# Feed-forward steps in another order, and three weight units cast by one operation

## The chip, the cores and the metric

The kernel runs on one core of one Trainium2 chip. The time is that of one execution on the device, in microseconds; the median of three executions is given, and beside it one execution was recorded by the profiler.

## The reference

One encoder block for 256 tokens of 2048 channels, all in float32. Two branches (gated linear attention and a Hyena convolution) are computed from one input projection, gated, merged, projected and normalised. Then comes the part that matters here, a squared-ReLU MLP of width 8192 and a second normalisation:

```
h = _layernorm(DEEPNORM_ALPHA * h + mix, ln1_g[l], ln1_b[l])
ff = jnp.square(jax.nn.relu(h @ w_ff1[l])) @ w_ff2[l]
h = _layernorm(DEEPNORM_ALPHA * h + ff, ln2_g[l], ln2_b[l])
```

## The kernel before

All weights stream from HBM in blocks of 128 x 2048 float32 (1 MB). TensorE works in a reduced float32 format, so each operand is taken as a high part (a cast on ScalarE, `cast`, L1103) and a low part (raw minus high, on VectorE, `rest`, L1106), and a product is three matmuls: high by high, high by low, low by high. In the table of the profile these casts stand under L1104 and all VectorE operations of the stage under L1101, the lines of the two helpers.

The MLP's hidden width is taken in four quarters of 2048. `ff1_first` computes the first quarter of h @ w_ff1. `ff_pairs` (L1278) then runs 48 steps; step s does one block of w_ff1 for a later quarter (16 blocks of 128 hidden channels make one quarter) and one block of w_ff2 for the quarter before it. Product with w_ff2 goes by a Strassen-Winograd scheme on 2 x 2 blocks: seven products in place of eight. The seven accumulators `w` lie in seven of the eight PSUM banks for 8 steps each; then their sums are added to the result in SBUF (`take_sum`, L1251, on ScalarE for the first quarter's, else on VectorE), and when the quarters for one half of the columns are done, eight additions join them (`join_sums`, L1262). The eighth bank holds the ff1 result `f` of the step.

What a step works on:

- A block of w_ff2, in one of three tiles of a ring, is four units u0 to u3 of 512 columns. `plain_split` (L1156) takes the high and low part of u0 to u2 as they are (the names b_h, b_l). Then VectorE adds u0 += u3 and u3 = u0 + u1, and GpSimd issues two DMAs that accumulate into the tile: u1 += (u3's columns once more from HBM, L1169) and u2 += u3 (L1170). `pair_split` (L1183) splits units 0 and 3, `last_split` (L1187) units 1 and 2, which the DMAs have changed (into the spare columns of the two fa tiles). So each block gives seven weight pieces: three plain, two of the pair, two of the last.
- `form_products` (L1238) does the three matmuls per piece, against the seven forms of the hidden activations in the fa tiles.
- A block of w_ff1, in one of two `fraw` tiles, is split in two halves (`half_split`, L1201), whose 2 x 12 weight loads and matmuls, of 512 and 256 columns, go into `f` (L147, L151). `quad_sum` (L1109) adds the two parts of `f` into a tile of hidden activations, one such tile for two steps: ScalarE copies one part (f_l), VectorE adds. After the second step `squares` (L1117) applies ReLU and square on ScalarE.
- `forms` (L1123) makes the seven forms of one activation tile with their high and low parts: on VectorE a chain of small differences and low parts, on ScalarE three casts that wait for them. They overwrite the fa slots when the quarter that used them is done with that slot.

High and low tiles of weights rotate over three buffers, which pair, half 0 and half 1 take in turn; the tiles of the plain units, of the last units and the `f` bank exist once.

The order within a step is written out by hand: `pin` keeps the instructions of an engine in the order of the program text. What is not pinned (the loads, the joins, the rest) a scheduler places; on SP's queue stand by turns the ring load of block p, which waits for the low part of `last_split(p - 3)`, and the fraw load of block p, which waits for half 1 of block p - 2. `quad_sum` and `take_sum` have high priority. In step s the text goes: products of the three plain pieces; `plain_split(s + 1)`; products of the pair; f half 0; `half_split(s + 1, 0)`; `pair_split(s + 1)`; products of the last pieces of step s - 1; `last_split(s)`; the load of a ring tile; f half 1; `quad_sum`; `half_split(s + 1, 1)`, which also issues the load of the next fraw block; `forms` in steps 9 to 16 of each 16; `squares` in odd steps. Ring and fraw loads are issued on SP's queue, the accumulating DMAs on GpSimd's. A sum is taken directly behind the last matmuls of its accumulator, in `form_products`.

Of the kernel before, what the change touches and what calls it, by code (L numbers as in the profile page):

```python
# [9 lines left out]
F32 = mybir.dt.float32  # L10
# [6 lines left out]
P = 128  # L17
# [26 lines left out]
def block_kernel(  # L44
# [93 lines left out]
    def channel_psum(name):  # L138
        return psum_main(name).rearrange("p (a b) -> p a b", a=2)
# [109 lines left out]
    with tc.tile_pool(name="xp", bufs=1) as xp, tc.tile_pool(name="xq", bufs=1) as xq:  # L249
        def units(pool, tag, n, **kw):  # L250
            t = pool.tile([P, n, OPENING * P], F32R, tag=tag, name=f"open_{tag}", **kw)
            return lambda a, b: t[:, a:b].rearrange("p k (b j) -> p k b j", b=OPENING)
# [713 lines left out]
    rows1 = load_rows(0)  # L966
    turn_b, turn_i = dfth, dftl
    for i, t in ((0, turn_b), (1, turn_i)):
        raw = ep.tile([P, 1024], F32, tag="wx", name=f"turn{i}")[:, 0:512].rearrange("p (a b) -> p a b", b=P)
        nc.scalar.dma_start(raw, ln_turn[i])  # L970
        nc.scalar.copy(t, raw)
        if i == 0:
            nc.vector.tensor_tensor(t[32:64], raw[32:64], t[32:64].bitcast(F32), op=ALU.subtract)
# [7 lines left out]
    for g in range(3):  # L981
        pss = token_group(mT, f"wo{g}")
        for tb in range(NT):
            add_mix(pss[tb], tb, g * 512, 512)
    x0 = tuple(ep.tile([P, D], F32R, tag=t, name=t) for t in ("xh", "xl"))
    parts = resident([x0] + halves(ep, "f", "wr1"))
    pss = [[psum_main(f"wo3_{tb}{ch}") for ch in range(2)] for tb in range(NT)]
    column_products(pss, mT, [queue.popleft()], range(NT), 0)
# [40 lines left out]

    def begin_three():  # L1030
        blocks = [queue.popleft(), [], []]
        hx, lx = (ep.tile([P, D], F32R, tag=t, name=f"{t}_f") for t in ("xh", "xl"))
        at = 0
        for b in (1, 2):
            n = fetched[0]
            fetched[0] = n + 1
            raw = wp.tile([P, D], F32, tag="raw", bufs=3, name=f"raw{n}")
            nc.sync.dma_start(raw, wblk[n])
            for h in range(2):
                src = raw[:, h * 1024:(h + 1) * 1024]  # L1040
                if b + h == 2:
                    hi, lo = hx[:, at:at + 1024], lx[:, at:at + 1024]
                    at += 1024
                    with tc.issue_after(scaled[0].ins):
                        nc.scalar.copy(hi, src)
                    with tc.issue_after(turned[1][1].ins):
                        nc.vector.tensor_tensor(lo, src, hi.bitcast(F32), op=ALU.subtract)
                elif b == 1:
                    hi, lo = weight_half(n, h)
                    split_hi_lo(hi, lo, src)  # L1050
                else:
                    hi, lo = n, src
                blocks[b].append((hi, lo))
        begun = [(channel_psum(f"f0_{b // 2}_{b % 2}"), parts, 1 if b == 2 else 2) for b, parts in enumerate(blocks)]
        for at, size in CHUNKS:
            for ps, parts, n in begun:
                if at // P < 8 * n:
                    high_by_tokens(ps, hT, parts[at // 1024], range(at // P, (at + size) // P), slice(0, P))
        n, src = blocks[2][1]
        blocks[2][1] = weight_half(n, 1)  # L1060
        split_hi_lo(*blocks[2][1], src)
        fetch()
        return begun
# [11 lines left out]
    def fa_slot(i):  # L1075
        if fa[1] is None:
            fa[1] = ep.tile([P, 8192], F32R, tag="f", name="fa1")
        t = fa[i // 4][:, i % 4 * 1792:(i % 4 + 1) * 1792]
        return t.rearrange("p (h k j) -> p h k j", h=2, j=P)
# [9 lines left out]
    quad_tiles = [base.tile([P, 4, P], F32, tag=t, name=f"fr{i}") for i, t in enumerate(("dfth", "dftl", "sum"))]  # L1089
    quad_tiles += [ep.tile([P, 4, P], F32, tag=f"fr{i}", name=f"fr{i}") for i in (3, 4)]  # L1090

    def quads(i):
        return quad_tiles[i % 5]

    pinned = [False]

# [6 lines left out]
    def cast(hi, src):  # L1103
        return pin(nc.scalar.copy(hi, src))  # L1104

    def rest(lo, src, hi):  # L1106
        return VT(lo, src, hi.bitcast(F32), ALU.subtract)
# [6 lines left out]
            cast(low, ps[:, 1])  # L1114
            VT(dst, halves[0], halves[1], ALU.add)

    def squares(i):  # L1117
        q = quads(i)
        pin(nc.scalar.activation(q, q, AF.Relu))
        return pin(nc.scalar.activation(q, q, AF.Square))  # L1120


    def forms(i, plain=False):  # L1123
        q, slot = quads(i), fa_slot(i)
        hi, lo = slot[:, 0], slot[:, 1]
        if plain:
            cast(hi[:, 0:4], q)
            rest(lo[:, 0:4], q, hi[:, 0:4])
            return
        t = base.tile([P, 2, P], F32, tag="as", name=f"fw{i}")  # L1130
        cast(hi[:, 0:3], q[:, 1:4])
        VT(t, q[:, 0:1].broadcast_to([P, 2, P]), q[:, 1:3][:, ::-1], ALU.subtract)
        cast(hi[:, 3:5], t)
        VT(q[:, 0], q[:, 1], t[:, 0], ALU.subtract)
        rest(lo[:, 0:3], q[:, 1:4], hi[:, 0:3])
        VT(q[:, 2], q[:, 3], q[:, 0], ALU.subtract)
        cast(hi[:, 5:7], q[:, 0:3:2])
        rest(lo[:, 3:5], t, hi[:, 3:5])
        rest(lo[:, 5:7], q[:, 0:3:2], hi[:, 5:7])
# [4 lines left out]
            return fa_slot(kt // 2)[:, part, ((1, 0), (3, 2))[kt % 2][ts.start // P]]  # L1144

    SLOTS = 48

    def ring_load(p):
        nc.sync.dma_start(ring_tile(p), wblk[FF_PAIRS + 2 * p])
# [5 lines left out]

    def plain_split(p):  # L1156
        raw, n = ring_tile(p), FF_PAIRS + 2 * p
        hi = ep.tile([P, D], F32R, tag="xh", name=f"b_h{p}")
        lo = ep.tile([P, 1024], F32R, tag="wx", name=f"b_l{p}")
        u = units(raw)  # L1160
        at = slice(0, 1024), slice(1024, 1536)
        low = lo, hi[:, 1536:2048]
        for c in at:
            cast(hi[:, c], raw[:, c])
        for c, dst in zip(at, low):
            rest(dst, raw[:, c], hi[:, c])
        VT(u[0], u[0], u[3], ALU.add)
        VT(u[3], u[0], u[1], ALU.add)
        nc.gpsimd.dma_start(u[1], wblk[n, :, 1536:2048], accum_op=ALU.add)  # L1169
        nc.gpsimd.dma_start(u[2], u[3], accum_op=ALU.add)  # L1170
        h = units(hi)
        pieces_of[p, 0] = list(zip(h[:3], units(lo) + h[3:]))

    def split_units(p, kind, hi, lo, raw):
        by_unit = [t.rearrange("p (u c) -> p u c", c=512) for t in (hi, lo)]
# [7 lines left out]
    def pair_split(p):  # L1183
        hi, lo = weight_half(FF_PAIRS + 2 * p, 0)
        split_units(p, 1, hi, lo, raw_units(p)[:, 0:4:3])
# [52 lines left out]
    def form_products(pss, p, which, ks):  # L1238
        i = p % 8
        slot = fa_slot(i)  # L1240
        for k, (wh, wl) in zip(ks, pieces_of.pop((p, which))):
            ps, f = pss[k], FORM[k]
            sh, sl = slot[:, 0, f], slot[:, 1, f]
            pin(MM(ps, sh, wh, start=(i == 0), stop=False))  # L1244
            MM(ps, sh, wl, start=False, stop=False)  # L1245
            pin(MM(ps, sl, wh, start=False, stop=(i == 7)))  # L1246
        if i == 7:
            for k in ks:
                take_sum(p // 16, p // 8 % 2, k, pss[k])

# [27 lines left out]
    def ff_pairs():  # L1278
        pss = [psum_side(f"w{j}") if j not in (2, 3, 4) else psum_main(f"w{j}") for j in range(7)]
        joins = []  # L1280
        for s in range(SLOTS):
            more = s + 1 < SLOTS
            pinned[0] = True
            form_products(pss, s, 0, (0, 1, 2))
            if more:
                plain_split(s + 1)
            form_products(pss, s, 1, (3, 4))
            ps = channel_psum(f"f{s // 16 + 1}_{s % 16}")
            channel_products(ps, hT, half_parts.pop((s, 0)), range(8))
            if more:  # L1290
                half_split(s + 1, 0)
                pair_split(s + 1)
            if s:
                form_products(pss, s - 1, 2, (5, 6))
                if s == SLOTS - 8:
                    joins = join_sums(0)
            last_split(s)
            if s + 2 < SLOTS:
                ring_load(s + 2)
            channel_products(ps, hT, half_parts.pop((s, 1)), range(8, 16))  # L1300
            i, c = divmod(s % 16, 2)
            quad_sum(i, c, ps, f"f{s // 16 + 1}_l{s % 16}")
            if more:
                half_split(s + 1, 1)
            if s >= 9 and (s - 9) % 16 < 8:
                forms((s - 9) % 16, s >= 2 * 16 + 9)
            if c:
                squares(i)
            if joins:
                joins.pop(0)()  # L1310
            pinned[0] = False
            if s == SLOTS - 2:
                stop_at[0] = nblk - 4
                fetched[0] = FF_PAIRS + 2 * SLOTS
            for _ in range(max(0, s - SLOTS + 3)):
                fetch()
        return pss, joins

    def ff_close(pss, joins):
        form_products(pss, SLOTS - 1, 2, (5, 6))  # L1320
        forms(7, True)
        for j in joins + join_sums(1):
            j()

# [25 lines left out]
    def quarters(*tiles):  # L1350
# [1 line left out]
        return [[(at[0], at[1]), (at[2], at[3])], [(at[4], at[5]), (at[6], at[7])]]  # L1352

    spare = [t[:, 7168:8192] for t in fa]
    own = [ep.tile([P, n], F32R, tag=t, name=f"{t}_r")
           for t, n in (("xh", D), ("xl", D), ("fraw", D))]
    parts = resident_pieces(quarters(*own, *spare)
                            + [[(a[:, c:c + 1024], b[:, c:c + 1024]) for c in (0, 1024)] for a, b in halves(ep, "hT", "wr3")])
    minus = ep.tile([P, P], F32, tag="minus", name="minus")
# [198 lines left out]
```

## Time and profile before

| | |
|---|---|
| median of 3 executions | 1818.28 us (1817.59 to 1818.85) |
| profiled execution | 1818.21 us |
| its span, first to last instruction | 1816.4 us |
| mean granted TensorE clock | 0.999 |
| ScalarE busy | 1042.5 us (57%) |
| GpSimd busy | 164.8 us (9%) |
| the 48 steps | from 1199.3 to 1717.4 us of the span |
| bytes moved | 424.77 MB, mean 234 GB/s |

A row of a timeline or of the chain gives a start and a duration in us, the engine, the line, the operation with its output and inputs, and in brackets the idle time before it with what ended it. PE is TensorE's matmuls, PEld its weight loads, DVE VectorE, ACT ScalarE, POOL GpSimd, SPq the queue that issues loads. A group row gives the count, busy us and mean ns of one, and behind the second bar the idle us before with what ended most of it. The matmuls of a step stand as w (L1244 to L1246) and f.

### The profile page before, as it was taken

What the parts mean: (1) busy time and instruction counts of PE and PEld (TensorE: products, weight loads), DVE (VectorE), ACT (ScalarE), POOL (GpSimd) and SP (SyncE); (2) the same over time, 40 slices, a digit from 0 to 9 for tenths busy, and PEclk for the clock granted to TensorE, in tenths of its full rate; (3) what the DMA queues carried; (4) which work ended last, traced back from release to release, by engine and by line L of the source; (5) the groups of instructions that cost most, each with busy time, mean ns of one, the idle gap of its engine ahead of it and who ended that gap; (6) DMA issues with size and microseconds to landing.
All of it is one profiled execution on the core that took longest, in us unless ns stands there. A gap on an engine that the chain in (4) does not pass through costs nothing.

```text
span 1816.4 us, 23481 instructions
## 1 busy us (share of the span) xinstructions
PE 1797.7 (99%) x8787; PEld 1505.1 (83%) x8787; DVE 1454.9 (80%) x1893; ACT 1042.5 (57%) x1423; POOL 164.8 (9%) x217
## 2 busy tenths in 40 slices
PE   9999999999999999999999999999999999999998
PEld 7888888888888888888888889888877887788887
DVE  6789887875689899988755667688889888989867
ACT  6678668865344444444544445666666566666632
POOL 1011110000111101010000000011111111111100
PEclk9999999999999999999999999999999999999999
DMA  8678876445798979797555764578777977789663
GB/s 324 227 256 292 249 230 200 149 163 204 229 297 250 308 248 283 251 278 258 197 187 186 310 235 159 187 213 248 236 227 235 275 235 221 221 255 273 214 219 127
DMA packets 79283, 424.77 MB, mean 234 GB/s; under 512 B 9817, under 2 KB 12393, under 8 KB 38465
## 3 DMA queue, kind: packets, MB, share of 16 engines
q1 hardware_dynamic: 47808, 336.61, 50.5%
q0 software_dynamic: 24304, 66.99, 18.2%
q10 hardware_dynamic: 7056, 19.67, 3.1%
q8 instruction: 69, 1.13, 0.3%
q14 instruction: 46, 0.37, 0.1%
HBM read 381.86 MB, written 16.25 MB: 219 GB/s over the span
## 4 chain that ended last, share of the span: by engine, by line
PE 87%; DVE 7%; ACT 3%; issue 3%; DMA 1%; ACTq 0%; DVEq 0%; POOL 0%
PE f L147 9%; PE f L151 5%; PE g L200 3%; PE g L199 3%; PE g L201 3%; PE ux L199 3%; PE ux L200 3%; PE ux L201 3%; PE w L1245 3%; PE w L1244 3%; PE w L1246 3%; PE k L147 2%; PE v L201 2%; PE v L200 2%; PE v L199 2%
## 5 line engine op out<-in xcount | busy, mean ns | idle before, releaser
L86 ACT CAST whi<-raw 128x1024 fp32r<-128x1024 f32 x392 | 412.7, 1055 | 408.6 <-PE ux L201 84.4
L87 DVE TENSOR_TENSOR wlo<-raw,whi 128x1024 fp32r<-128x1024 f32 x392 | 477.1, 1221 | 206.8 <-ACT whi L86 205.5
L147 PE MATMUL f<-hT,whi 128*128 128x512 f32 x984 | 246.4, 395 | 2.4 <-DVE fr L1101 1.9
L147 PEld LDWEIGHTS f<-hT,whi 128*128 128x128 f32 x984 | 180.4, 189 | 44.4 <-DVE fr L1101 10.1
L151 PEld LDWEIGHTS f<-hT,wlo 128*128 128x128 f32 x984 | 132.3, 190 | 8.7
L151 PE MATMUL f<-hT,wlo 128*128 128x256 f32 x984 | 135.0, 282 | 0.0
L1101 DVE TENSOR_TENSOR wlo<-fraw,whi 128x1024 fp32r<-128x1024 f32 x96 | 117.0, 1219 | 11.8 <-ACT whi L1104 11.8
L1169 POOL DMA_DIRECT2D ring<-wblk x48 | 41.7, 869 | 723.0 <-DVE ring L1101 723.0
L1104 ACT CAST whi<-ring 128x1024 fp32r<-128x1024 f32 x48 | 50.6, 1054 | 90.6 <-DVE ring L1101 83.8
L1104 ACT CAST whi<-fraw 128x1024 fp32r<-128x1024 f32 x96 | 100.7, 1049 | 0.2 <-PE f L147 0.2
L200 PE MATMUL g<-wlo,xT 128*128 128x512 f32 x256 | 100.1, 391 | 0.0
L201 PE MATMUL ux<-whi,xT 128*128 128x512 f32 x256 | 99.9, 390 | 0.0
L201 PE MATMUL g<-whi,xT 128*128 128x512 f32 x256 | 99.8, 390 | 0.0
L200 PE MATMUL ux<-wlo,xT 128*128 128x512 f32 x256 | 99.6, 389 | 0.0
L199 PE MATMUL g<-whi,xT 128*128 128x512 f32 x256 | 93.8, 392 | 0.0
L199 PE MATMUL ux<-whi,xT 128*128 128x512 f32 x256 | 89.7, 389 | 0.0
L1101 DVE TENSOR_TENSOR b_l<-ring,b_h 128x1024 fp32r<-128x1024 f32 x48 | 58.7, 1224 | 33.1 <-ACT b_h L1104 33.0
L1104 ACT CAST b_h<-ring 128x1024 fp32r<-128x1024 f32 x96 | 74.9, 829 | 8.8 <-ACT whi L1104 8.2
L1101 DVE TENSOR_TENSOR ring<-ring 128x512 f32<-128x512 f32 x96 | 66.0, 688 | 1.6
L1101 DVE TENSOR_TENSOR wlo<-ring,whi 128x1024 fp32r<-128x1024 f32 x48 | 58.8, 1225 | 2.7 <-ACT whi L1104 1.2
L1101 DVE TENSOR_TENSOR fa<-ring,fa 128x1024 fp32r<-128x1024 f32 x48 | 58.5, 1219 | 0.8 <-ACT fa L1104 0.8
L1104 ACT COPY f_l<-f 128x256 f32<-128x256 f32 x64 | 23.7, 370 | 61.1 <-PE f L147 58.2
(538 smaller groups left out, 4345.4 us busy)
## 6 DMA issues: line engine op xcount, KB each, us to landing
raw<-wblk SPq DMA_DIRECT2D x204, 1024.0 KB, 5.1
fraw<-wblk SPq DMA_DIRECT2D x48, 1024.0 KB, 7.1
ring<-wblk SPq DMA_DIRECT2D x48, 1024.0 KB, 6.2
Td<-T POOLq DMA_DIRECT2D x32, 384.0 KB, 5.4
conv_sb<-conv_rows SPq DMA_DIRECT2D x12, 1024.0 KB, 11.5
Tl<-Td POOLq DMA_DIRECT2D x16, 768.0 KB, 9.4
ring<-wblk POOLq DMA_DIRECT2D x48, 256.0 KB, 4.3
ring<-ring POOLq DMA_DIRECT2D x48, 256.0 KB, 5.0
```

The costliest lines, as they stand in the source:

```text
L86: return (nc.scalar.copy(hi, src), nc.vector.tensor_tensor(lo, src, hi.bitcast(F32), op=ALU.subtract))
L87: nc.vector.tensor_tensor(lo, src, hi.bitcast(F32), op=ALU.subtract))
L147: MM(ps[:, :, ts], hi[:, js], act[:, kt, :, ts], start=(kt == 0 and opens), stop=(kt == KT - 1))
L151: MM(ps[:, 0, ts], lo[:, js], act[:, kt, 0, ts], start=False, stop=False)
L199: MM(pss[tb], sh, wh, start=(kt == 0), stop=False)
L200: MM(pss[tb], sh, wl, start=False, stop=False)
L201: MM(pss[tb], sl, wh, start=False, stop=(kt == KT - 1))
L1101: return pin(nc.vector.tensor_tensor(dst, a, b, op=op))
L1104: return pin(nc.scalar.copy(hi, src))
L1244: pin(MM(ps, sh, wh, start=(i == 0), stop=False))
L1245: MM(ps, sh, wl, start=False, stop=False)
L1246: pin(MM(ps, sl, wh, start=False, stop=(i == 7)))
```

## The change

In a step the last pieces of step s - 1 are now multiplied directly behind the pair's, and both halves of f follow. Splitting goes in the order of use: plain units of step s + 1, last units of step s, pair of s + 1, half 0, half 1. The text of the ring load stands ahead of `plain_split`; the scheduler puts it on SP's queue as in the kernel before, for ring tile s + 3 as soon as VectorE has done the low part of `last_split(s)`, which was the tile's last reader, and the fraw load of block s + 3 next, behind half 1 of block s + 1. `squares` stand in even steps ahead of `forms`; `forms` of a quarter's eight tiles go, by the table FORMED, in the steps 9, 10, 12, 14, 15, 17, 18 and 20 counted from the start of a quarter, in place of 9 to 16, and those that fall behind the last step run in `ff_close`. Both stand ahead of `quad_sum` and half 1. Sums are no longer taken in `form_products` but by `take_sums`, behind the splits. The plain units' high and low part lie in one tile of 3072 columns (12 KB per partition), each made by one operation of 1536 columns where there were two, of 1024 and 512. The tile tags at other places follow: the first normalisation's two turn loads use the tag fraw, and tiles with the tag xh are made 3072 wide and cut to 2048.

```diff
@@ -1089,8 +1089,9 @@
     quad_tiles = [base.tile([P, 4, P], F32, tag=t, name=f"fr{i}") for i, t in enumerate(("dfth", "dftl", "sum"))]
     quad_tiles += [ep.tile([P, 4, P], F32, tag=f"fr{i}", name=f"fr{i}") for i in (3, 4)]
 
-    def quads(i):
-        return quad_tiles[i % 5]
+
+    def quads(n):
+        return quad_tiles[n % 5]
 
     pinned = [False]
 
@@ -1114,20 +1115,20 @@
             cast(low, ps[:, 1])
             VT(dst, halves[0], halves[1], ALU.add)
 
-    def squares(i):
-        q = quads(i)
+    def squares(n):
+        q = quads(n)
         pin(nc.scalar.activation(q, q, AF.Relu))
         return pin(nc.scalar.activation(q, q, AF.Square))
 
 
-    def forms(i, plain=False):
-        q, slot = quads(i), fa_slot(i)
+    def forms(n):
+        q, slot, plain = quads(n), fa_slot(n % 8), n >= 24
         hi, lo = slot[:, 0], slot[:, 1]
         if plain:
             cast(hi[:, 0:4], q)
             rest(lo[:, 0:4], q, hi[:, 0:4])
             return
-        t = base.tile([P, 2, P], F32, tag="as", name=f"fw{i}")
+        t = base.tile([P, 2, P], F32, tag="as", name=f"fw{n}")
         cast(hi[:, 0:3], q[:, 1:4])
         VT(t, q[:, 0:1].broadcast_to([P, 2, P]), q[:, 1:3][:, ::-1], ALU.subtract)
         cast(hi[:, 3:5], t)
@@ -1144,6 +1145,7 @@
             return fa_slot(kt // 2)[:, part, ((1, 0), (3, 2))[kt % 2][ts.start // P]]
 
     SLOTS = 48
+    FORMED = {16 * (q - 1) + s: 8 * q + i for q in range(1, 4) for i, s in enumerate((9, 10, 12, 14, 15, 17, 18, 20))}
 
     def ring_load(p):
         nc.sync.dma_start(ring_tile(p), wblk[FF_PAIRS + 2 * p])
@@ -1155,21 +1157,16 @@
 
     def plain_split(p):
         raw, n = ring_tile(p), FF_PAIRS + 2 * p
-        hi = ep.tile([P, D], F32R, tag="xh", name=f"b_h{p}")
-        lo = ep.tile([P, 1024], F32R, tag="wx", name=f"b_l{p}")
+        t = ep.tile([P, 3072], F32R, tag="xh", name=f"b{p}")
+        hi, lo = t[:, 0:1536], t[:, 1536:3072]
         u = units(raw)
-        at = slice(0, 1024), slice(1024, 1536)
-        low = lo, hi[:, 1536:2048]
-        for c in at:
-            cast(hi[:, c], raw[:, c])
-        for c, dst in zip(at, low):
-            rest(dst, raw[:, c], hi[:, c])
+        cast(hi, raw[:, 0:1536])
+        rest(lo, raw[:, 0:1536], hi)
         VT(u[0], u[0], u[3], ALU.add)
         VT(u[3], u[0], u[1], ALU.add)
         nc.gpsimd.dma_start(u[1], wblk[n, :, 1536:2048], accum_op=ALU.add)
         nc.gpsimd.dma_start(u[2], u[3], accum_op=ALU.add)
-        h = units(hi)
-        pieces_of[p, 0] = list(zip(h[:3], units(lo) + h[3:]))
+        pieces_of[p, 0] = list(zip(units(hi), units(lo)))
 
     def split_units(p, kind, hi, lo, raw):
         by_unit = [t.rearrange("p (u c) -> p u c", c=512) for t in (hi, lo)]
@@ -1244,7 +1241,9 @@
             pin(MM(ps, sh, wh, start=(i == 0), stop=False))
             MM(ps, sh, wl, start=False, stop=False)
             pin(MM(ps, sl, wh, start=False, stop=(i == 7)))
-        if i == 7:
+
+    def take_sums(pss, p, ks):
+        if 0 <= p < SLOTS and p % 8 == 7:
             for k in ks:
                 take_sum(p // 16, p // 8 % 2, k, pss[k])
 
@@ -1280,32 +1279,36 @@
         joins = []
         for s in range(SLOTS):
             more = s + 1 < SLOTS
+            n, c = divmod(s + 16, 2)
             pinned[0] = True
             form_products(pss, s, 0, (0, 1, 2))
+            form_products(pss, s, 1, (3, 4))
+            if s:
+                form_products(pss, s - 1, 2, (5, 6))
+            ps = channel_psum(f"f{s // 16 + 1}_{s % 16}")
+            for h in range(2):
+                channel_products(ps, hT, half_parts.pop((s, h)), range(8 * h, 8 * h + 8))
+            if s + 2 < SLOTS:
+                ring_load(s + 2)
             if more:
                 plain_split(s + 1)
-            form_products(pss, s, 1, (3, 4))
-            ps = channel_psum(f"f{s // 16 + 1}_{s % 16}")
-            channel_products(ps, hT, half_parts.pop((s, 0)), range(8))
+            take_sums(pss, s, (0, 1, 2))
+            last_split(s)
+            if more:
+                pair_split(s + 1)
+            take_sums(pss, s, (3, 4))
             if more:
                 half_split(s + 1, 0)
-                pair_split(s + 1)
-            if s:
-                form_products(pss, s - 1, 2, (5, 6))
-                if s == SLOTS - 8:
-                    joins = join_sums(0)
-            last_split(s)
-            if s + 2 < SLOTS:
-                ring_load(s + 2)
-            channel_products(ps, hT, half_parts.pop((s, 1)), range(8, 16))
-            i, c = divmod(s % 16, 2)
-            quad_sum(i, c, ps, f"f{s // 16 + 1}_l{s % 16}")
+            if c == 0 and s:
+                squares(n - 1)
+            if FORMED.get(s, 0) >= 8:
+                forms(FORMED[s])
+            take_sums(pss, s - 1, (5, 6))
+            quad_sum(n, c, ps, f"f{s // 16 + 1}_l{s % 16}")
             if more:
                 half_split(s + 1, 1)
-            if s >= 9 and (s - 9) % 16 < 8:
-                forms((s - 9) % 16, s >= 2 * 16 + 9)
-            if c:
-                squares(i)
+            if s == SLOTS - 7:
+                joins = join_sums(0)
             if joins:
                 joins.pop(0)()
             pinned[0] = False
@@ -1314,11 +1317,15 @@
                 fetched[0] = FF_PAIRS + 2 * SLOTS
             for _ in range(max(0, s - SLOTS + 3)):
                 fetch()
+        squares(31)
         return pss, joins
 
     def ff_close(pss, joins):
         form_products(pss, SLOTS - 1, 2, (5, 6))
-        forms(7, True)
+        take_sums(pss, SLOTS - 1, (5, 6))
+        for s in range(SLOTS, SLOTS + 8):
+            if s in FORMED:
+                forms(FORMED[s])
         for j in joins + join_sums(1):
             j()
```

More of the change, by code (lines that the diff above doesn't have):

```diff
@@ L968, in block_kernel @@
     for i, t in ((0, turn_b), (1, turn_i)):
-        raw = ep.tile([P, 1024], F32, tag="wx", name=f"turn{i}")[:, 0:512].rearrange("p (a b) -> p a b", b=P)
+        raw = ep.tile([P, D], F32, tag="fraw", name=f"turn{i}")[:, 0:512].rearrange("p (a b) -> p a b", b=P)
         nc.scalar.dma_start(raw, ln_turn[i])
@@ L984, in block_kernel @@
             add_mix(pss[tb], tb, g * 512, 512)
-    x0 = tuple(ep.tile([P, D], F32R, tag=t, name=t) for t in ("xh", "xl"))
+    x0 = tuple(ep.tile([P, n], F32R, tag=t, name=t)[:, 0:D] for t, n in (("xh", 3072), ("xl", D)))
     parts = resident([x0] + halves(ep, "f", "wr1"))
@@ L1031, in begin_three @@
         blocks = [queue.popleft(), [], []]
-        hx, lx = (ep.tile([P, D], F32R, tag=t, name=f"{t}_f") for t in ("xh", "xl"))
+        hx, lx = (ep.tile([P, n], F32R, tag=t, name=f"{t}_f") for t, n in (("xh", 3072), ("xl", D)))
         at = 0
@@ L1354, in block_kernel @@
     spare = [t[:, 7168:8192] for t in fa]
-    own = [ep.tile([P, n], F32R, tag=t, name=f"{t}_r")
-           for t, n in (("xh", D), ("xl", D), ("fraw", D))]
+    own = [ep.tile([P, n], F32R, tag=t, name=f"{t}_r")[:, 0:D] for t, n in (("xh", 3072), ("xl", D), ("fraw", D))]
     parts = resident_pieces(quarters(*own, *spare)
```

## The prediction

> Times in one step are given as t, in us after its first matmul (w<-b_h, L1244).
>
> **What bounds the kernel now.** First the page: TensorE.
>
> ```profile
> span 1816.4 us, 23481 instructions
> PE 1797.7 (99%) x8787; PEld 1505.1 (83%) x8787; DVE 1454.9 (80%) x1893; ACT 1042.5 (57%) x1423; POOL 164.8 (9%) x217
> ```
>
> The profiled run took 1818.21 us, 1.8 outside this span; the median is 1818.28, so the sum can be made on the profiled run as it stands. PE's 99% hides waits, because a matmul that waits for its weight load counts as busy. So I go next to the chain that ended last, which in the MLP's 48 steps shows either PE or VectorE.
>
> ```profile
> 1216.97 1.84 PE f L147 x8
> ...
> 1299.75 1.85 PE f L147 x8
> ...
> 1313.80 1.22 DVE fa L1101
> ...
> 1324.84 1.22 DVE fa L1101
> ...
> 1337.06 1.22 DVE fa L1101
> ...
> 1402.78 1.84 PE f L147 x8
> ...
> 1475.21 1.85 PE f L147 x8
> ...
> 1591.11 1.84 PE f L147 x8
> ...
> 1632.50 1.84 PE f L147 x8
> ...
> 1653.65 1.84 PE f L147 x8
> ```
>
> The rows on f are the second ff1 half of steps 1, 9, 18, 25, 35, 39 and 41; those on fa are the `last` low part of steps 11 to 13. The first 8 steps, dense, take 82.78: one every 10.345 us. From 1299.75 to 1402.78 lie 9 steps: 103.03 − 93.10 = 9.93 us too many. From 1475.21 to 1591.11 lie 10 (step 25 to 35): 115.90 − 103.45 = 12.45. From 1632.50 to 1653.65 lie 2: 0.46. **All that this change can win is therefore 22.8 us**: a ceiling at 1795.4. The excess stands where `forms` run (steps 9 to 16 and 25 to 32) and the quarter's sums are taken; there the period is 11.04 or 12.22, VectorE is on the chain, and every second step is longer. The table by stage gives its busy time:
>
> ```profile
> 1249.69:1260.04 10.35, 10.35 (x55) 8.86 (x53) 8.39 (x10) 5.95 (x7) 1.75 (x2) 1.00 0.88 256
> 1322.48:1333.52 11.04, 10.94 (x54) 8.69 (x53) 9.08 (x15) 8.01 (x12) 1.78 (x2) 1.00 0.78 240
> 1333.52:1345.72 12.20, 11.21 (x54) 8.70 (x53) 11.36 (x18) 6.86 (x10) 1.76 (x2) 1.00 0.72 218
> ```
>
> The columns are span, PE, PEld, DVE, ACT, POOL, clock, DMA share, GB/s. VectorE is busy 8.4 us of a plain step and (9.08 + 11.36) / 2 = 10.2 of one with `forms`, less than 10.345. So the loss is not work but VectorE standing idle in its turn; the waits of stage 1197 to 1720 say for what:
>
> ```profile
> L1101 DVE TENSOR_TENSOR b_l<-ring,b_h 128x1024 fp32r<-128x1024 f32 x47 | 57.5, 1224 | 33.1 <-ACT b_h L1104 33.0
> L1101 DVE TENSOR_TENSOR wlo<-fraw,whi 128x1024 fp32r<-128x1024 f32 x96 | 117.0, 1219 | 11.8 <-ACT whi L1104 11.8
> L147 PEld LDWEIGHTS f<-hT,whi 128*128 128x128 f32 x776 | 142.2, 190 | 37.0 <-DVE fr L1101 10.1
> L1245 PEld LDWEIGHTS w<-wlo,fa 128*128 128x128 f32 x96 | 18.0, 187 | 15.6 <-DVE wlo L1101 12.2
> ```
>
> **The change part by part.** *One operation for three units.* Two casts and two low parts of 1024 and 512 columns become one each.
>
> ```profile
> L1101 DVE TENSOR_TENSOR b_h<-ring,b_h 128x512 fp32r<-128x512 f32 x47 | 32.2, 684 | 0.0
> L1104 ACT CAST b_h<-ring 128x1024 fp32r<-128x1024 f32 x47 | 49.0, 1042 | 8.8 <-ACT whi L1104 8.2 <-ACT zr L1104 0.3 <-ACT fa L1104 0.2
> L1104 ACT CAST b_h<-ring 128x512 fp32r<-128x512 f32 x47 | 28.9, 615 | 0.0
> ```
>
> No row has 1536 columns. On VectorE 512 more columns cost 1224 − 684 = 540 ns, so 1536 take an estimated 1.76; two operations overlap their ends and took from 1253.06 to 1254.80 (timeline, below), 1.74. On ScalarE 1042 + 427 = 1.47, against at most 1.66 for the pair. Busy time is level within 0.1 a step. What moves is the start of the low part: it now waits for the whole cast, 1.47 after the cast's start instead of 1.04, 0.43 later. Bounds: −0.1 to +0.43 in each of the 24 or so steps where VectorE is behind, −2 to +10 us over the kernel. I take it in as the b wait of 0.4 in each of the 16 `forms` steps (below), 6.4, and none in the others, where the cover hides it.
>
> *The order.* A plain step of before:
>
> ```profile
> 1249.69 0.39 PE L1244 MATMUL w<-b_h,fa 128*128 128x512 f32 x1
> ...
> 1252.50 0.33 SPq L1197 DMA_DIRECT2D fraw<-wblk  x1
> ...
> 1252.86 0.39 PE L1246 MATMUL w<-whi,fa 128*128 128x512 f32 x1
> ...
> 1253.06 1.23 DVE L1101 TENSOR_TENSOR b_l<-ring,b_h 128x1024 fp32r<-128x1024 f32 x1 [0.59 <-ACT b_h L1104]
> ...
> 1254.80 1.42 DVE L1101 TENSOR_TENSOR ring<-ring 128x512 f32<-128x512 f32 x2
> ...
> 1256.92 0.87 POOL L1169 DMA_DIRECT2D ring<-wblk  x1 [8.37 <-DVE ring L1101]
> ...
> 1257.46 1.22 POOL L1170 DMA_DIRECT2D ring<-ring  x1
> 1257.49 1.05 ACT L1104 CAST fa<-ring 128x1024 fp32r<-128x1024 f32 x1
> ...
> 1258.57 1.23 DVE L1101 TENSOR_TENSOR fa<-ring,fa 128x1024 fp32r<-128x1024 f32 x1
> ...
> 1259.82 0.33 SPq L1149 DMA_DIRECT2D ring<-wblk  x1
> ```
>
> From 1249.69 to 1252.86 are 14 matmuls, 0.226 each, so 21 take 4.75 and the two ff1 halves the other 5.6, in either order: TensorE's own work costs nothing either way. In after TensorE has w0–2 until t = 2.03, w3–4 until 3.4, w5–6 until 4.75, f until 10.3. ScalarE then does the b cast from 2.25 (its tile is read until 2.03) to 3.7, `last` from 5.0 (its tile is read by w5–6) to 6.0, pair, half 0, squares; VectorE the b low part to 5.45, the two adds to 6.85, `last` to 8.0, pair to 9.2, half 0 to 10.4, then `forms`, the f sum, half 1. Due times: pair at 2.05 of the next step (3.2 us of cover), `last` at 3.4, half 0 at 4.75, and the f sum at 4.75, where it was 3.4 before. `Forms` and squares stand behind everything that the next matmuls need, and every second or third step has none to make up in. A `forms` step costs VectorE its 10.2 and two waits (half 1 some 0.5 behind its cast, b some 0.4): 11.0, 0.7 over. Eight of them in steps 9 to 20, and seven sums at about 0.68, are 5.6 + 4.8 = 10.4; less 3.2 of cover leaves 7.2 a quarter. The four plain steps between can give back 1.0 each (8.4 + 0.9 = 9.3 of 10.345): 3.2 left. So with transfers as fast as now the excess would be about 2 × 3.2, and following the queues instruction by instruction I get 4 to 5.
>
> SP's loads move. `fraw` goes with half 1, t = 2.8 to 3.5. The ring load goes behind `last`, which is now ahead of pair and half 0: from t = 10.13 (1259.82) to 8.05. The two accumulates are issued behind the adds: acc2 (L1170) was at 7.77, now 8.1. So **the ring load leaves together with the accumulates instead of 2.4 us behind them**. And what waits for them moves the other way: the `last` cast of the next step goes from 7.80 to 5.0. From issue to need there were 10.345 + 0.03 = 10.4 us, now 10.345 + 5.0 − 8.1 = 7.2. Behind that cast stand ScalarE's pair, half 0, the form casts and f_l, and so VectorE. How long are they under way? The page's median, and two single cases, each by the issues and the landings that the trace gives for its stretch:
>
> ```profile
> ring<-ring POOLq DMA_DIRECT2D x48, 256.0 KB, 5.0
> ```
>
> ```profile
> 1470.09 0.33 SPq L1197 DMA_DIRECT2D fraw<-wblk  x1
> ...
> 1474.34 1.22 POOL L1170 DMA_DIRECT2D ring<-ring  x1
> ```
>
> ```profile
> fraw<-wblk SPq DMA_DIRECT2D x1, 1024.0 KB, 7.1
> ```
>
> ```profile
> ring<-ring POOLq DMA_DIRECT2D x1, 256.0 KB, 7.4
> ```
>
> ```profile
> ring<-wblk SPq DMA_DIRECT2D x1, 1024.0 KB, 7.9
> fraw<-wblk SPq DMA_DIRECT2D x1, 1024.0 KB, 9.4
> ```
>
> ```profile
> ring<-ring POOLq DMA_DIRECT2D x1, 256.0 KB, 9.2
> ```
>
> The median is 5.0, with the next load 2.4 us behind. The acc2 issued at 1474.34 had a `fraw` load that left 4.25 before it and landed 1470.09 + 7.1 = 2.85 after: 7.4, 2.4 longer. The one of the last two fences left at 1412.32, with a ring load (1406.33) landing 1.9 and a `fraw` (1407.80) landing 4.9 after it: 9.2, 4.2 longer. In after every acc2 has a ring load beside it for its whole flight and a `fraw` issued 4.6 before: between 7.4 and 9.2, nearer the first, since the two loads are further apart (4.55 us instead of 2.7). I take 7.8. Then VectorE cannot catch up: from the adds of one step to the `last` low part of the next it waits for 1.24 (add's end 1256.22 to issue 1257.46) + 7.8 + 1.05 (cast) = 10.1, and a plain step takes that, giving back 0.2, not 1.0. **The excess is 2 × 7.2 = 14.4; the gain 22.8 − 14.4 = 8.4; 1818.2 − 8.4 = 1810.**
>
> The Trainium skill speaks against the change here: DMA: Bandwidth & Descriptors, Queues, rings and completion order, says that each DMA engine takes turns between its queues packet by packet, so that a load from SP holds up an accumulate from POOL as long as both have packets. The rows of 7.4 and 9.2 agree. By that rule alone acc2 would be later by the load's whole time on the engines, an estimate near 8 us, the same side of 7.2.
>
> The tiles' renaming I cost at nothing: the turn's two loads are issued before the MLP begins, the b tile was single before too, and TensorE has read it by t = 2.03, ahead of the next cast. The joins' 0.46, now behind the f sum, I count as gone.
>
> **The rivals.** *A: the accumulates stay at 5 to 6.5*, because loads that are further apart don't pile up. For it: most acc2 of before had a load in flight at one end and still took 5.0. Then the plain steps give back, the excess is 4 to 5, and the time 1818.2 − 22.8 + 4.5 = 1800. *B, slower: the accumulate's landing becomes the bound.* From 8.05 on (10.345 − 2.3) a plain step too is longer than TensorE's and loses instead of giving back; each 0.25 more costs between 2 (8 plain steps among the 24) and 6 us (all 24), I take 3. With 14.4 at 8.05 the excess passes 22.8 at 8.05 + 0.25 × 8.4 / 3 = 8.75: above that landing the change is slower. At the 9.2 of the last row the excess is 14.4 + 13.8 = 28, the time 1823.5. For it: that row, and `last` and the accumulates then run in lockstep. Against: where `last` waits, the ring load behind it waits too and moves away from the accumulates. *C: the single cast of 1536.* At its upper end, 10 instead of 6.4, it adds 4 us: 1814 with slow accumulates, at the edge of 0.2%; below nothing, 8 us less, between the forecast and A. That the order isn't as written, I give nothing: squares and `forms` stand in the queues as named.
>
> **How the numbers follow.** Forecast (acc2 7.2 to 8.2; 1805 to 1814): 0.40. A: 0.15. C, or acc2 8.2 to 8.75 (1814 to 1819): 0.22. B: 0.23. A difference under 0.2%, 3.6 us, is about what a measurement of this kernel can't tell from none: faster is below 1814.6. Faster 0.40 + 0.15 = 0.55 less a little for slow ends, 0.53; same 0.24 (C and the near end of B); slower 0.23. The range goes from A to B's price: 1799 to 1823.
>
> **What would show it.** Right: the 11.04 and 12.2 periods gone or near 10.7; the acc2 landing 7 to 8 us; a wait of the `last` cast for DMA ring<-ring, now nearly none; PEld's wait for wlo from 12.2 to under 6. A would show acc2 at 5 and the `last` cast waiting for PE w. B would show `last` waiting over 1 us for the DMA in most steps, also in plain ones, and periods over 10.345 there. Wrong altogether would be a stall at f for the f sum (L147 <- fr), now 10 us of waiting, grown; or the b low part's wait for its cast, now 33.0, on the chain.

## The result and the profile after

The changed kernel takes 1840.62 us (1839.36 to 1841.35, four runs) against 1817.99 beside it: a ratio of 1.0123, 95% interval 1.0106 to 1.0141, 22.6 us slower. The forecast was 1810.

The page of the changed kernel, span and busy time, with PE's two lines of the costliest groups:

```profile
span 1839.2 us, 23248 instructions
PE 1798.7 (98%) x8787; PEld 1506.2 (82%) x8787; DVE 1453.8 (79%) x1845; ACT 1036.1 (56%) x1375; POOL 164.9 (9%) x217
...
L147 PE MATMUL f<-hT,whi 128*128 128x512 f32 x984 | 244.9, 393 | 12.8 <-DVE fr L1102 12.8
L147 PEld LDWEIGHTS f<-hT,whi 128*128 128x128 f32 x984 | 180.0, 189 | 53.4 <-DVE fr L1102 18.8
```

No engine has more work to speak of: VectorE and ScalarE are busy 1 and 6 us less, TensorE 1 more, and the span has grown by 22.8. TensorE waits more for the f sum (12.8 us where it was 1.9), which alone would point at `forms`. The summary of waits between 1197 and 1745 us (engine, line, releaser: total, times, longest) names something that the kernel before hardly had:

```profile
ACT fa L1105 <- DMA ring<-ring: 100.1, 23, 7.8
DVE fa L1102 <- ACT fa L1105: 63.0, 22, 5.3
```

In before the first of these was 1.0 us, once. The cast of the last units waits 23 times, 4.4 us in the mean, for the second accumulate (acc2), and VectorE stands 63 us behind it. The page's table of DMA issues says why, in its last column, the median us to landing:

```profile
fraw<-wblk SPq DMA_DIRECT2D x48, 1024.0 KB, 5.6
ring<-wblk SPq DMA_DIRECT2D x48, 1024.0 KB, 7.2
...
ring<-wblk POOLq DMA_DIRECT2D x48, 256.0 KB, 5.5
ring<-ring POOLq DMA_DIRECT2D x48, 256.0 KB, 8.4
```

acc2 went from 5.0 to 8.4, the first accumulate (acc1) from 4.3 to 5.5, the ring load from 6.2 to 7.2; only `fraw` came down, 7.1 to 5.6. But a median hides the shape. Of 47 landings 12 took 6 us or less and 14 took 9.5 or more. The timeline around steps 14 and 15 (start, length, engine; the bracket is idle time and its releaser) shows one of each kind:

```profile
1347.76 0.87 POOL L1167 DMA_DIRECT2D ring<-wblk  x1 [13.49 <-issue]
...
1348.24 0.33 SPq L1151 DMA_DIRECT2D ring<-wblk  x1
1348.30 1.22 POOL L1168 DMA_DIRECT2D ring<-ring  x1
...
1352.06 0.33 SPq L1194 DMA_DIRECT2D fraw<-wblk  x1
...
1352.32 0.39 PE L1243 MATMUL w<-fa,fa 128*128 128x512 f32 x1
...
1355.68 0.87 POOL L1167 DMA_DIRECT2D ring<-wblk  x1 [6.16 <-issue]
1356.22 1.22 POOL L1168 DMA_DIRECT2D ring<-ring  x1
1359.10 1.05 ACT L1105 CAST fa<-ring 128x1024 fp32r<-128x1024 f32 x1 [7.38 <-DMA ring<-ring]
...
1360.18 1.22 DVE L1102 TENSOR_TENSOR fa<-ring,fa 128x1024 fp32r<-128x1024 f32 x1 [5.04 <-ACT fa L1105]
```

The landings of that stretch, acc1, ring load and acc2, as the trace gives them:

```profile
ring<-wblk POOLq DMA_DIRECT2D x1, 256.0 KB, 7.6
ring<-wblk SPq DMA_DIRECT2D x1, 1024.0 KB, 6.6
ring<-ring POOLq DMA_DIRECT2D x1, 256.0 KB, 10.7
```

The three leave within 0.54 us. acc1 lands at 1347.76 + 7.6 = 1355.4, half a microsecond behind the ring load (1348.24 + 6.6 = 1354.8); acc2 is caught by the `fraw` load of 1352.06 as well and lands at 1359.0. ScalarE has stood for it 7.38 us, with the pair's cast and all else behind it.

The trace of before held this case once, just ahead of the steps. The accumulates of block 0 had a ring load right behind them, and landed as late:

```profile
1188.02 0.90 POOL L1169 DMA_DIRECT2D ring<-wblk  x1 [289.12 <-DVE ring L1101]
1188.58 1.24 POOL L1170 DMA_DIRECT2D ring<-ring  x1
1188.64 0.33 SPq L1149 DMA_DIRECT2D ring<-wblk  x1
```

```profile
ring<-wblk POOLq DMA_DIRECT2D x1, 256.0 KB, 7.6
ring<-ring POOLq DMA_DIRECT2D x1, 256.0 KB, 9.2
```

Since in the changed kernel the ring load waits for the low part of `last`, the stall holds it back too: in its timeline above the accumulates of 1355.68 have no ring load beside them and landed 5.9 and 6.5 us later. So steps come in turns, one dense and one long, by the table by stage (span, PE, PEld, DVE, ACT, POOL, clock, DMA share, GB/s):

```profile
1347.79:1358.12 10.33, 10.33 (x55) 8.86 (x54) 7.29 (x8) 3.93 (x5) 3.48 (x4) 1.00 0.88 246
1358.12:1372.40 14.28, 12.50 (x55) 9.92 (x54) 11.33 (x16) 10.30 (x14) 0.45 (x1) 0.88 0.65 191
```

Added up over steps 1 to 46, the excess over 10.345 us is 22.9 in before and 45.1 in after: the 22 us that were lost. The granted clock of 0.88 in the second row stands in two steps of after (this one and step 39) and in one of before (step 32). It is worth an estimated (1 − 0.88) × 14.28 = 1.7 us in such a step, so about that much of the 22. The chain that ended last reaches back only to 1635 us in after (11% of the span), and goes through the transfer itself:

```profile
1674.09 11.59 DMA ring<-ring
1685.78 1.05 ACT fa L1105
1686.85 1.01 DVE fa L1102
...
1697.34 9.58 DMA ring<-ring
```

### The profile page after: what moved, and what is told of

It reads as the page before. It is cut to its first block, busy times and chain, and to the rows that moved or that the text cites. A ratio compares the mean times of both kernels' runs of the same rounds, so it can differ in the third digit from the quotient of the medians.

```text
span 1839.2 us, 23248 instructions
## 1 busy us (share of the span) xinstructions
PE 1798.7 (98%) x8787; PEld 1506.2 (82%) x8787; DVE 1453.8 (79%) x1845; ACT 1036.1 (56%) x1375; POOL 164.9 (9%) x217
## 5 line engine op out<-in xcount | busy, mean ns | idle before, releaser
L87 DVE TENSOR_TENSOR wlo<-raw,whi 128x1024 fp32r<-128x1024 f32 x392 | 477.4, 1221 | 206.0 <-ACT whi L86 204.4
L147 PE MATMUL f<-hT,whi 128*128 128x512 f32 x984 | 244.9, 393 | 12.8 <-DVE fr L1102 12.8
L147 PEld LDWEIGHTS f<-hT,whi 128*128 128x128 f32 x984 | 180.0, 189 | 53.4 <-DVE fr L1102 18.8
L151 PEld LDWEIGHTS f<-hT,wlo 128*128 128x128 f32 x984 | 126.1, 191 | 4.8
L151 PE MATMUL f<-hT,wlo 128*128 128x256 f32 x984 | 127.7, 283 | 0.0
L1102 DVE TENSOR_TENSOR wlo<-fraw,whi 128x1024 fp32r<-128x1024 f32 x96 | 117.1, 1219 | 12.2 <-ACT whi L1105 12.2
L1105 ACT CAST fa<-ring 128x1024 fp32r<-128x1024 f32 x48 | 50.4, 1050 | 128.4 <-DMA ring<-ring 100.1
L1102 DVE TENSOR_TENSOR fa<-ring,fa 128x1024 fp32r<-128x1024 f32 x48 | 58.6, 1221 | 63.0 <-ACT fa L1105 63.0
L1102 DVE TENSOR_TENSOR b<-ring,b 128x1536 fp32r<-128x1536 f32 x48 | 84.2, 1755 | 9.2 <-ACT b L1105 8.7
L1105 ACT CAST b<-ring 128x1536 fp32r<-128x1536 f32 x48 | 71.1, 1481 | 5.2 <-ACT whi L1105 4.0
L1102 DVE TENSOR_TENSOR wlo<-ring,whi 128x1024 fp32r<-128x1024 f32 x48 | 58.6, 1221 | 0.9 <-ACT whi L1105 0.5
```

The lines of the kernel that those rows point to most:

```text
L147: MM(ps[:, :, ts], hi[:, js], act[:, kt, :, ts], start=(kt == 0 and opens), stop=(kt == KT - 1))
L151: MM(ps[:, 0, ts], lo[:, js], act[:, kt, 0, ts], start=False, stop=False)
L1102: return pin(nc.vector.tensor_tensor(dst, a, b, op=op))
```

## The experiments

The theory after the result: loads that take turns with the accumulates make these late, and the cast of the last units now needs them 3.2 us earlier, so it stalls ScalarE's queue. Rivals: the single operation of 1536 columns; the order itself (squares and forms ahead of the f sum). The median of before was 1817.9 to 1818.4 beside all the runs below.

**The ring load moved away (e1).** It goes out on ScalarE's queue, behind half 1's cast:

```diff
+    def ring_late(p):
+        pin(nc.scalar.dma_start(ring_tile(p), wblk[FF_PAIRS + 2 * p]))
...
-            if s + 2 < SLOTS:
-                ring_load(s + 2)
+            if s == 0:
+                ring_load(2)
...
                 half_split(s + 1, 1)
+            if s + 3 < SLOTS:
+                ring_late(s + 3)
```

> The changed kernel, but the ring load of block s + 3 is issued by ScalarE's queue behind the cast of half 1 (t about 1.6 of the next step), not by SP's together with the accumulates. Theory (the ring load beside the accumulates makes them land at 8.4 us, and ScalarE's cast of the last pieces waits for that): the second accumulate lands at 5 to 5.5 us at the median, the cast's 100 us of waiting for it go below 15, and the time falls to 1800 to 1808 us. Rival 1 (the single operations of 1536 columns cost the time): 1830 to 1841. Rival 2 (squares and forms ahead of the f sum cost it, whatever the transfers do): 1830 to 1841, with TensorE's waits for the f sum still near 30 us.

1835.16 us, ratio 1.0089 (1.0072 to 1.0106): a miss. The landings did improve where the load stayed away: 22 of 47 were at 6 us or less, in place of 12. But 14 waits were left, of 6 us each:

```profile
ACT fa L1105 <- DMA ring<-ring: 83.8, 14, 9.0
```

Because ScalarE's queue is the one that stalls, a load put in it slides with the stall. In the timeline of this run it is back between the two accumulates:

```profile
1344.70 0.86 POOL L1170 DMA_DIRECT2D ring<-wblk  x1 [13.46 <-DVE ring L1102]
...
1345.19 0.33 ACTq L1154 DMA_DIRECT2D ring<-wblk  x1
1345.24 1.22 POOL L1171 DMA_DIRECT2D ring<-ring  x1
```

**Two operations again (e2), and the single one alone (e3).** e2 is the changed kernel with the casts and low parts of 1024 and 512 columns; e3 is the kernel before with the single operation and its tile.

```diff
-        cast(hi, raw[:, 0:1536])
-        rest(lo, raw[:, 0:1536], hi)
+        at = slice(0, 1024), slice(1024, 1536)
+        for c in at:
+            cast(hi[:, c], raw[:, c])
+        for c in at:
+            rest(lo[:, c], raw[:, c], hi[:, c])
```

> The changed kernel with the plain units' cast and low part as two operations each, of 1024 and 512 columns, as before. Theory (accumulates): 1836 to 1843, the cast of the last pieces waits for the accumulate as long as with one operation. Rival 1 (the operations of 1536 columns): 1818 to 1830. Rival 2: 1836 to 1843.

> The kernel before, in its own order, with the single operations of 1536 columns and the tile of 12 KB alone. Theory (accumulates): 1816 to 1823, since the loads keep their places. Rival 1: 1828 to 1841. Rival 2: 1816 to 1823.

e2: 1837.99 (1.0109; 1.0094 to 1.0124). e3: 1825.72 (1.0042; 1.0027 to 1.0057). So the single operation costs some 2.6 us in the changed order, where the two intervals overlap, and 7.4 in the old one, where its low part's wait for the cast rose from 33 us to this:

```profile
DVE b L1101 <- ACT b L1104: 48.5, 37, 2.1
```

It is a real loss, between the two expectations of e3, but a third of the whole at most.

**No accumulates (e4), no ring loads (e7), no fraw loads (e8).** Each leaves one kind of transfer out of the changed kernel (e7 from block 3 on, e8 inside the steps), so none of the three computes the reference's output.

```diff
-        nc.gpsimd.dma_start(u[1], wblk[n, :, 1536:2048], accum_op=ALU.add)
-        nc.gpsimd.dma_start(u[2], u[3], accum_op=ALU.add)
```

```diff
-            if s + 2 < SLOTS:
+            if s == 0:
                 ring_load(s + 2)
```

```diff
-        if h and p + 2 < SLOTS:
-            block_load(p + 2)
```

> The changed kernel without the two accumulating DMAs of each step (this leaves out the additions to the last two units, so the product with w_ff2 is not the reference's); all else stands. Theory (accumulates): the waits of the cast of the last pieces are gone and the time is 1797 to 1805. Rival 1 and rival 2: 1825 to 1841.

> The changed kernel without the ring loads from block 3 on (this leaves out weights of w_ff2, so the output is not the reference's); both accumulates stay. Theory (the load beside the accumulates makes them late): the second lands at 4.7 to 5.5 us at the median, the cast's waits are under 10 us, the time is 1799 to 1806 us. Rival (slow by themselves): 8 us as now, 1830 to 1841.

> The changed kernel without the loads of the w_ff1 blocks inside the steps (this leaves out weights of w_ff1, so the output is not the reference's); ring loads and accumulates stay. Theory: the first accumulate still lands near 7.6 and the second near 8.4 where the ring load leaves within 0.6 us of them, those near 10 are gone: 1810 to 1828 us. Rival (the ring load alone makes the whole loss): 1835 to 1841. Rival (the fraw loads alone): 1799 to 1806.

e4: 1800.29 (0.9902; 0.9887 to 0.9917). e7: 1799.42 (0.9899; 0.9885 to 0.9914). e8: 1822.26 (1.0025; 1.0014 to 1.0036). With both accumulates in place but no ring load, the accumulates land as they did before; the page of e7:

```profile
ring<-wblk POOLq DMA_DIRECT2D x48, 256.0 KB, 4.2
ring<-ring POOLq DMA_DIRECT2D x48, 256.0 KB, 4.9
```

and the cast waits 8.1 us for them in all. The order, the single operation and the accumulates are all there, and the whole loss is gone: it takes the ring load's company. Without `fraw` acc2's median is still 8.3, but only 2 landings instead of 14 exceed 9.5, and the time falls by 18 us. So the ring load makes the accumulates late, and the fraw load on top makes the long ones. With accumulates or ring loads away, TensorE's weight loads wait 4.3 or 4.4 us for the f sum in place of 18.8: that wait was a consequence.

**The last units behind half 0 (e5).**

```diff
             take_sums(pss, s, (0, 1, 2))
-            last_split(s)
             if more:
                 pair_split(s + 1)
             take_sums(pss, s, (3, 4))
             if more:
                 half_split(s + 1, 0)
+            last_split(s)
```

> The changed kernel with the split of the last units moved behind half 0 on ScalarE and VectorE (pair, half 0, last), all else as changed. Its cast is then due some 4 us later in the step, and the ring load goes out 2.3 us later too. Theory (loads take turns with the accumulates, and the cast of the last units comes too early for that): the cast's waits for the accumulate fall from 100 us to under 15, at the price of VectorE's wait for the pair's cast, about 1 us in a step: 1804 to 1814 us. Rival (the accumulates are slow by themselves in this order, or the stall is the f sum's): 1825 to 1841.

1826.06 (1.0045; 1.0030 to 1.0060). Half of the expectation held: acc2 is back at 5.0, and no wait of the cast for it is left. The price was too low. With `last` no longer between, VectorE comes to the pair's low part ahead of the pair's cast, and this group of waits grows from 12.2 to

```profile
DVE wlo L1102 <- ACT whi L1105: 61.9, 71, 1.5
```

which in the steps with forms makes periods of 10.8 to 10.9.

**acc2 as an operation (e6, f1, f2, f3).** VectorE adds u2 += u3 in place of the DMA (e6); the same with two operations for the plain units (f1); GpSimd adds (f2); f1 with e1's ring load (f3).

```diff
         VT(u[3], u[0], u[1], ALU.add)
+        VT(u[2], u[2], u[3], ALU.add)
         nc.gpsimd.dma_start(u[1], wblk[n, :, 1536:2048], accum_op=ALU.add)
-        nc.gpsimd.dma_start(u[2], u[3], accum_op=ALU.add)
```

In f2 the added line is `pin(nc.gpsimd.tensor_tensor(u[2], u[2], u[3], op=ALU.add))`.

> The changed kernel with u2 += u3 done by VectorE (512 columns, 0.6 us more a step) in place of the second accumulating DMA. Only the first is left, issued 0.54 us earlier and with half the packets of the two. Theory: it lands at 4 to 5.5 us where no load is beside it and near 7.6 where the ring load is, against 7.8 us of time; waits under 25 us, and VectorE's 0.6 us costs 8 to 12 us in the steps with forms: 1804 to 1816 us. Rival (the stall isn't the accumulates' landing): 1830 to 1850.

> The version with u2 += u3 on VectorE and, beside it, the plain units' cast and low part as two operations again. If the operation of 1536 columns costs by the later start of its low part, then most where VectorE is the bound (7.4 us in the old order) and less where the accumulates were (2.6 us in the changed order): here, with the accumulates out of the way, 3 to 7 us less than with one operation, 1804.5 to 1808.5 us. If it costs only in the old order: 1811 to 1812.5.

> The version with u2 += u3 taken from VectorE and given to GpSimd, whose engine is nearly idle. No run has shown such an operation's length. If it runs beside VectorE undisturbed and ends within some 5 us: VectorE is 0.6 us a step shorter, 1801 to 1808 us. If it holds up VectorE for its own length, or comes too late for the cast of the last units: 1812 to 1830.

> VectorE's add, two operations for the plain units, and the ring load on ScalarE's queue behind half 1's cast. Only the first accumulate is left and the ring load is mostly away from it. If what still holds the version with VectorE's add is the ring load beside the first accumulate: 1 to 4 us below the same without the move (that one is f1_add_two). If it is VectorE's own work: level with it within 1.5 us.

e6: 1811.59 (0.9966; 0.9953 to 0.9978). **f1: 1805.90 (0.9931; 0.9919 to 0.9944), the fastest version that leaves nothing out**, 12 us below before. f3: 1806.33 (0.9933; 0.9920 to 0.9947), level with f1, so what is left there is not the ring load. f2: 1819.93 (1.0010; 1.0002 to 1.0019). In f1 one 256 KB accumulate a step is left, and its wait is nearly gone:

```profile
ACT fa L1105 <- DMA ring<-wblk: 5.0, 2, 3.5
```

e6 minus f1, 5.7 us, prices the single operation a third time.

**Forms in eight steps on end (f4),** on e6:

```diff
-    FORMED = {16 * (q - 1) + s: 8 * q + i for q in range(1, 4) for i, s in enumerate((9, 10, 12, 14, 15, 17, 18, 20))}
+    FORMED = {16 * (q - 1) + s: 8 * q + i for q in range(1, 4) for i, s in enumerate(range(9, 17))}
```

> The version with u2 += u3 on VectorE, with forms in eight steps on end (9 to 16) as in the kernel before, in place of 9, 10, 12, 14, 15, 17, 18, 20. The prediction counted 1 us of catching up in each of the four plain steps between, 8 us over two quarters. If that holds: 1815 to 1822 us. If the spreading does nothing: 1810.5 to 1813.

1827.03 (1.0048; 1.0036 to 1.0061): the spreading is worth 15.4 us here, twice what was counted.

## Why the prediction was wrong, point by point

- **The bound and the ceiling** held. Without accumulates or without ring loads the new order takes 1800.3 and 1799.4, at rival A's 1800, and keeps 4.5 us of the excess over steps 1 to 46, where 4 to 5 was read for transfers as fast as before. The order does what the queues were read to do.
- **The single operation of 1536 columns:** its lengths were right (1.76 and 1.47 estimated; the groups have 1755 and 1481 ns), and so was the kind of loss, a later low part. Counted at 6.4, it measured 7.4 (e3), 5.7 (e6 less f1) and 2.6 us (e2), least where VectorE was waiting for something else.
- **Forms spread over twelve steps:** counted as 1.0 us given back in each plain step, 8 in all; f4 measured 15.4, on e6. Right in kind, half in size.
- **"I take 7.8" is the step that failed, together with the price put on what lies above it.** The ring load beside the accumulates was seen, and the rows of 7.4 and 9.2 bounded the median of 8.4. The two accumulates of block 0 in the trace of before, with the ring load right behind them, are not in it, nor is one acc2 of that trace that took 10.6 us (issued at 1655.29). And the choice of the nearer row rested on fraw being 4.6 us older, while the case to fear was the ring load in flight from the first packet and the *next* fraw load arriving ahead of the end: 14 of 47 landings were outside both rows, up to 11.6. The sum then used one constant landing and let a late one cost only the catching up; "each 0.25 more costs … I take 3" gives 14.4 + 3 × 0.35 / 0.25 = 18.6 for the median of 8.4, that is 1814. Measured was 45.1. As a price: slow landings were to cost 14.4 − 4.5 = 9.9 us, and by e7 they cost 1840.6 − 1799.4 = 41.2. A landing that comes too late stops the whole ScalarE queue: pair, half 0, forms and f sum. A mean of short and long landings is not the cost of the mean.
- **"now 10.345 + 5.0 − 8.1 = 7.2"**, the time from issue to need, was mis-sized too. In steps 4 to 8, where VectorE is not behind, it was 7.0 to 7.2 as forecast. Where it is behind, its adds and with them the accumulates go out 2 us and more later in the step, while TensorE's reading of the tile does not move: in the timeline of step 14 from 1348.30 to the last w matmul's end at 1352.71, 4.4 us. Of the 14 landings over 9.2 us, 13 were issued so late, with 4.0 to 6.1 us left. A landing of 10 is then not 2.8 but some 5.6 us over.
- **"Where `last` waits, the ring load behind it waits too and moves away"** was true and counted on the wrong side. So not every acc2 has a ring load beside it. The landing does not settle at a middle value; the delay makes a good landing after each bad one, and the bad one is paid in full.
- **Rival B** comes nearest, but not by its own mechanism. It let plain steps lose from a landing of 8.05 on; in steps 4 to 8, which are plain, acc2 took 7.9 to 9.1 us and the period stayed at 10.33. By the order of the queues the adds of the next step stand ahead of `last` and do not wait for it, so that the 10.1 us of the sum are not the length of a step; this is argued, not tested. The loss came where VectorE was behind, and there the break-even of 8.75 was too high: at a median of 8.4 the change already lost 22.6 us. The sentence drawn from the Trainium skill (DMA: Bandwidth & Descriptors, Queues, rings and completion order), by which the accumulate shares packet turns with the load for the load's whole time, gave an estimate near 8; the traces agree: acc1 lands within 0.7 us of the ring load's end in 18 of the 19 steps in which the two leave within 0.7 us of each other, and at 4.2 without it.
- **Rival C** is real but small: e2 shows some 2.6 of 22.6 us.
- What stays open is the exact share of the two halves of the cause, later landing and earlier need. e5 restores both at once, e7 only the landing; the earlier need with a slow landing is the changed kernel, and the old need with a slow landing was not tried.

## What to carry to other kernels

When an edit moves a transfer, list what else is in flight from its issue to its landing, and for each small transfer that something waits for, compare the time left with its *contended* landing, not the median. Take the time left from the steps in which the issuing engine is late. When a wait heads an in-order queue, price it by everything behind it and by its worst cases, one by one. A small transfer that must beat bulk loads may be better as an engine's operation: 0.7 us of VectorE in each step (mean 692 ns in e6) bought 29 us (1840.6 to 1811.6).

## What the runs showed of the hardware

- An accumulate of 256 KB took 4.2 us with no ring load beside it (acc1 in e7, median) and 7.6 with one that left 0.5 us later (the rows of after). In the 19 steps of after in which a 1 MB ring load left 0.4 to 0.7 us behind acc1, acc1 landed between 1.4 us before the load's end and 0.7 behind it, acc2 0.9 to 4.2 behind it.
- How near the load must be shows in after too: acc2 took 4.9 to 5.1 us in the three steps in which the ring load left 1.9 us behind it, and 7.6 and 7.7 in the two in which it left 1.5 behind it.
- GpSimd's add of 512 float32 columns is no free help. In f2 the timeline has it beside VectorE:

```profile
1256.02 1.22 DVE L1102 TENSOR_TENSOR fa<-ring,fa 128x1024 fp32r<-128x1024 f32 x1
...
1256.35 2.06 POOL L1167 TENSOR_TENSOR ring<-ring 128x512 f32<-128x512 f32 x1 [7.43 <-DVE ring L1102]
1257.22 2.27 DVE L1102 TENSOR_TENSOR wlo<-ring,whi 128x1024 fp32r<-128x1024 f32 x1
...
1258.35 0.84 POOL L1168 DMA_DIRECT2D ring<-wblk  x1
```

VectorE's next low part takes 2.27 us instead of 1.22: it ends 1.08 after GpSimd's operation (1258.41), about its own length. The Trainium skill (SBUF — State Buffer, SBUF: two separate sides) says that a VectorE operation with two SBUF inputs and a GpSimd operation that reads SBUF block each other for a whole instruction; these rows agree. The move took 0.7 us from VectorE's work and gave 0.8 back (mean 2036 ns of the pair's low part against 1221). It also holds up what stands behind it in GpSimd's queue: acc1 leaves only at 1258.35, when the add is about done, and the cast of the last units waits for it, 1.6 us in all in e6 and 52.7 in f2:

```profile
ACT fa L1105 <- DMA ring<-wblk: 52.7, 19, 5.0
```
